# Seven block products of sums in place of eight, for six pairs of token tiles of an output product

## The chip, the cores and the metric

The kernel runs on one core of a Trainium2 chip. The metric is the device time of one execution in microseconds (us); lower is better. The engines are named as in the profile: PE (TensorE), DVE (VectorE), ACT (ScalarE), POOL (GpSimd) and SP (SyncE, which here issues nearly all DMA transfers).

## What is computed

Two request groups (1024 tokens each, width 1024) go through one encoder layer with shared weights:

```python
proj = x @ w_in                      # x: layer norm of the input
q_da, k_da, v_da, g_da, b_cv, c_cv, h_cv, g_cv, q_mx, g_mx = jnp.split(proj, idx, axis=-1)
o_da = diff_attention(q, k, v, lam, lam_init, subln_g) * jax.nn.silu(g_da)
o_cv = b_cv * short_conv(c_cv * h_cv, conv_w) * jax.nn.silu(g_cv)
o_mx = memory_attention(q_mx, mem, w_mem_kv) * jax.nn.silu(g_mx)
out = jnp.concatenate([o_da, o_cv, o_mx], axis=-1) @ w_o
return layer_norm(ALPHA * x + out, ln_g, ln_b)
```

The change is about the last two lines: the product of the mixed heads (1024 tokens x 1024, per group) with `w_o` (1024 x 1024), the residual, and the closing layer norm.

## The kernel before

Every product is taken in three passes over operands split into a high part (fp32r) and a low part (what the high part leaves out): high x high, high x low, low x high. A token tile is 128 rows, a column half 512, and a contraction block (kb) 128.

The program is written out by hand in one order. `Flow` keeps a planned clock: each piece of PE work adds its estimate with `fl.pe(ns)`, and `after(ns, fn)` puts work of the other engines into the program when that clock has come far enough. Each engine's queue then holds its instructions in the order in which they were put there. Twenty attention jobs (two groups x four heads and one memory attention x two query halves) form the frame. Between their steps the `Fillers` list supplies the projection tiles (`pQ`, `pK`, `pV`, `pG`, ... at L435 to L437), and at its end the output products. PE has eight PSUM banks: four for scores and transposes, two that the fillers take in turn (`next_bank`), one for small extras (`bank`), one for the attention output (`po`).

The output part before (L866 to L956):

- `load_wo(n, gap)` fetches column half n of `w_o` in eight blocks `woraw`. POOL makes the high part `woh` (L157), DVE the low part `wol` (L160). Half 0 is loaded in the last job, half 1 when the last projection tile is done.
- `Out(g, t)` is one token tile; there are sixteen. `load` fetches the mixed heads `mraw` (512 KB) and the input rows `xr` (512 KB), both through SP. `prepare` splits `mraw` (ACT `mixh` at L908, DVE `mixl`). `residual` makes ALPHA times the normed input: ACT at L915, DVE at L916, two adds on POOL at L919.
- `passes(n, kb)` issues three matmuls 128x128 by 128x512 into `pout` (L927): 8 blocks x 2 halves x 3 = 48 per tile, 768 in all. After a half, DVE adds the residual (L930) and takes `bn_stats` (L933).
- `finish` closes a tile: DVE `bn_aggr` (L941), POOL the reciprocal root in two small operations (L943, L944), DVE `centre` (L948) and `scale` (L951) for each half, and the store, through SP for the first four tiles and through ACT's queue for the others.

```python
for ti, (a, b) in enumerate(((self.mh, wh), (self.mh, wl), (self.ml, wh))):
    T.matmul(self.ps, a[:, kb, :], b, start=kb == 0 and ti == 0, stop=kb == KB - 1 and ti == 2)
```

## Time and profile before

| | |
|---|---|
| time, median of 3 runs (lowest to highest) | 1214.94 us (1214.8 to 1216.38) |
| profiled execution, its own time | 1216.07 us |
| span of the profiled execution, first to last instruction | 1214.2 us |
| mean granted TensorE clock over the span | 0.996 of 2.4 GHz |
| busy: PE, DVE, ACT, POOL | 1175.9, 803.0, 426.2, 415.7 us |
| DMA | 182.61 MB, mean 150 GB/s |

PE is busy for 97% of the span, so the place to look at is the 3% in which it is not, and the number of matmuls. A page's busy times say how much an engine did; whether its work costs time is told by the idle time of PE and by what ended it.

### The profile page before, as it was taken

The numbers are of one execution on the slowest core, as the hardware profiler recorded it, in microseconds if no ns is written. First come the engines' busy times: TensorE is split into PE (matmuls) and PEld (weight loads), VectorE is DVE, ScalarE is ACT, GpSimd is POOL, SyncE is SP. The second block draws the span as 40 slices with busy tenths as digits, with TensorE's granted clock in tenths as the row PEclk, the third lists the DMA queues.
The fourth block names the chain that finished last, engine by engine and source line by source line (L and its number), as shares of the span: only waits on it lengthen the run. The fifth ranks groups of instructions, "written<-read, shape, count | busy, mean of one in ns | idle before, by whom it ended". The sixth has DMA issues, their size and how long they took to land.

```text
span 1214.2 us, 15653 instructions
## 1 busy us (share of the span) xinstructions
PE 1175.9 (97%) x5881; PEld 922.0 (76%) x5881; DVE 803.0 (66%) x1156; ACT 426.2 (35%) x703; POOL 415.7 (34%) x466
## 2 busy tenths in 40 slices
PE   8899999999999999999999999999999998899997
PEld 6677777777777777788777777777777877788885
DVE  4779857666677675543766765665655456887776
ACT  4624333334233334334344333433433344111220
POOL 4754423352234430322311113023110346445443
PEclk9999999999999999999999999999999999999999
DMA  8366336433644389753321212312322368354341
GB/s 325 102 230 217 145 130 208 153 144 113 216 156 156 122 281 309 260 191 128 133 71 64 92 40 95 100 68 92 111 78 74 127 222 294 99 196 144 133 145 52
DMA packets 83644, 182.61 MB, mean 150 GB/s; under 512 B 7713, under 2 KB 26353, under 8 KB 83441
## 3 DMA queue, kind: packets, MB, share of 16 engines
q1 hardware_dynamic: 80112, 175.33, 41.3%
q10 hardware_dynamic: 3456, 6.29, 1.3%
q8 instruction: 46, 0.75, 0.3%
q14 instruction: 30, 0.24, 0.1%
HBM read 119.69 MB, written 61.91 MB: 150 GB/s over the span
## 4 chain that ended last, share of the span: by engine, by line
PE 75%; DVE 11%; POOL 3%; issue 3%; ACT 3%; DMA 3%; SPq 0%; POOLq 0%; DVEq 0%; ACTq 0%
PE pout L927 13%; PE ps L678 7%; PE pt L736 5%; PE po L764 3%; PE pG L435 2%; PE po L766 2%; PE po L765 2%; PE pG L437 2%; PE pG L436 2%; DVE mx L685 2%; PE pQ L435 2%; PE pQ L437 2%; PE pQ L436 2%; ACT e L686 2%; PE pV L435 2%
## 5 line engine op out<-in xcount | busy, mean ns | idle before, releaser
L686 ACT ACTIVATE e<-ps,mx 128x1024 f32<-128x1024 f32 x128 | 142.8, 1116 | 295.8 <-DVE mx L685 295.6
L685 DVE TENSOR_REDUCE mx<-ps 128x1 f32<-128x1024 f32 x128 | 150.6, 1218 | 87.7 <-PE ps L678 87.7
L160 DVE TENSOR_TENSOR tl<-pt,th 128x1024 fp32r<-128x1024 f32 x80 | 97.3, 1217 | 11.7 <-ACT th L742 11.6
L927 PE MATMUL pout<-woh,mixh 128*128 128x512 f32 x256 | 100.6, 393 | 0.0
L927 PE MATMUL pout<-woh,mixl 128*128 128x512 f32 x256 | 100.4, 392 | 0.0
L927 PE MATMUL pout<-wol,mixh 128*128 128x512 f32 x256 | 100.2, 391 | 0.0
L742 ACT ACTIVATE th<-pt 128x1024 fp32r<-128x1024 f32 x80 | 82.3, 1029 | 42.6 <-PE pt L736 42.1
L694 DVE SCALAR_TENSOR_TENSOR e<-e,ssum,e 128x1024 f32<-128x1024 f32 x64 | 87.9, 1373 | 0.0
L919 POOL TENSOR_TENSOR xr<-xr,lnrow 128x512 f32<-128x512 f32 x32 | 55.7, 1758 | 68.9 <-DVE xr L916 68.8
L476 POOL TENSOR_TENSOR sw<-sw,ropet 128x512 f32<-128x512 f32 x32 | 41.7, 1302 | 90.7 <-DVE sw L470 88.1
L736 PE MATMUL pt<-ident,e 128*128 128x128 f32 x512 | 66.8, 274 | 4.8 <-ACT e L686 4.8
L736 PEld LDWEIGHTS pt<-ident,e 128*128 128x128 f32 x512 | 58.9, 141 | 16.1 <-ACT e L686 8.1
L678 PE MATMUL ps<-kh,qh 64*128 64x512 f32 x256 | 62.8, 444 | 5.4 <-DVE tl L160 5.4
L722 POOL TENSOR_SCALAR em<-em,rm 128x256 f32<-128x256 f32 x64 | 31.9, 517 | 83.2 <-DVE rm L720 76.4
L160 DVE TENSOR_TENSOR wl<-wraw,wh 128x1024 fp32r<-128x1024 f32 (+1 forms) x33 | 43.0, 1303 | 23.7 <-POOL wh L157 13.8
L908 ACT ACTIVATE mixh<-mraw 128x1024 fp32r<-128x1024 f32 x16 | 17.0, 1061 | 114.6 <-PE pout L927 97.6
L764 PE MATMUL po<-th,vh 128*128 128x512 f32 x128 | 56.7, 443 | 0.0
L927 PEld LDWEIGHTS pout<-woh,mixl 128*128 128x128 f32 x256 | 48.3, 189 | 10.8 <-DVE mixl L160 0.6
L678 PE MATMUL ps<-kl,qh 64*128 64x512 f32 x256 | 54.6, 392 | 1.6 <-DVE kl L479 1.5
L927 PEld LDWEIGHTS pout<-wol,mixh 128*128 128x128 f32 x256 | 48.4, 189 | 10.0
L927 PEld LDWEIGHTS pout<-woh,mixh 128*128 128x128 f32 x256 | 48.4, 189 | 9.9
L678 PE MATMUL ps<-kh,ql 64*128 64x512 f32 x256 | 53.9, 390 | 0.0
(284 smaller groups left out, 3069.9 us busy)
## 6 DMA issues: line engine op xcount, KB each, us to landing
wp<-w SPq DMA_DIRECT2D x80, 512.0 KB, 4.3
wraw<-in_wt SPq DMA_DIRECT2D x32, 512.0 KB, 4.4
w<-wh SPq DMA_DIRECT2D x28, 512.0 KB, 5.4
w<-wl SPq DMA_DIRECT2D x28, 512.0 KB, 3.8
mraw<-mix SPq DMA_DIRECT2D x16, 512.0 KB
xr<-in_x SPq DMA_DIRECT2D x16, 512.0 KB, 6.5
out<-xr ACTq DMA_DIRECT2D x24, 256.0 KB, 2.1
x<-in_x SPq DMA_DIRECT2D x8, 512.0 KB, 4.4
```

What stands on the lines that cost most here:

```text
L160: (eng or V).tensor_tensor(out, x, hi.bitcast(F32), op=ALU.subtract)
L435: T.matmul(ps, wh[:, k], hh, start=kb == 0, stop=False)
L436: T.matmul(ps, wh[:, k], hl, start=False, stop=False)
L678: T.matmul(ps[c][:, n], q[r, qt * P:(qt + 1) * P], k[r, n], start=i == 0, stop=i == 2)
L685: V.tensor_reduce(mx[:, c:c + 1], ps[c], AX.X, ALU.max, negate=True)
L686: A.activation(e[c], ps[c], AF.Exp, bias=mx[:, c:c + 1], accum_out=sm[:, c:c + 1])
L694: V.scalar_tensor_tensor(e[0], e[1], st, e[0], op0=ALU.mult, op1=ALU.add)
L736: T.transpose(pt[:, u * HS + i * P:u * HS + (i + 1) * P], self.tiles[i][:, (b + u) * P:(b + u + 1) * P], const["ident"])
L742: A.activation(th, pt, AF.Copy)
L764: T.matmul(self.po, vh[:, k, :], th[:, c], start=k == 0, stop=False)
L919: after(2200 + 2000 * n, lambda c=c: G.tensor_tensor(xt[:, c], xt[:, c], ab[:, c], op=ALU.add))
L927: T.matmul(self.ps, a[:, kb, :], b, start=kb == 0 and ti == 0, stop=kb == KB - 1 and ti == 2)
```

## The change

The first four token tiles of group 0 keep the old form. The other twelve are taken as six pairs. With the 2 x 2 blocks A11, A12 (first tile, contraction halves), A21, A22 (second tile) and B11 to B22 (quarters of `w_o`), a pair needs seven block products P0 to P6 of twelve matmuls each, four of them with sums of blocks:

- `Pair.ORDER` names the seven products, operand, bank and, where there is one, the sum of `w_o` blocks: P0 A11 x B11 into bank `pa`; P1 S12 x T1 into `pb`; P2 A12 x B21 into `pa` again; P3 S12 x T0 into `pc`; P4 S34 x T2 into `pd`; P5 S34 x B22 into `pc`; P6 A22 x T3 into `pd`.
- P0 alone is needed too, so ACT copies `pa` to `s1` before P2 goes on adding into that bank. ACT also copies `pc` to `s5` after P3. DVE and POOL put the results together in `xr`.
- The sums of the token blocks are made by POOL (`sums`), their splits by ACT and DVE (`splits`), for the next pair during the present one.
- The sums of the `w_o` blocks, and the split quarters of `w_o`, are made in the course of jobs 11 and later by POOL (`park_wo`, `park_unit`) and parked in DRAM; `load_wo` and `load_sums` fetch both parts, with no split. The residuals are made there too and parked (`park_residual`).
- The closing norm of a pair's second tile (`mixed`) is done in one ACT pass with a scale and a bias (POOL makes the bias `nbo` in two more small operations), a multiply on DVE and an add on POOL. The last pair's second tile has the old form.
- Stores go through SP, but for the last pair's.

```diff
+RP = 162000
...
+    def park_unit(n, x, dst):
+        hi = sb([P, HS], F32R, ("kmh", "kml")[n % 2], "whi")
+        hi_of(hi, x)
+        after(300, lambda: G.tensor_tensor(x, x, hi.bitcast(F32), op=ALU.subtract))
+        def out():
+            dma(dst[0], hi.bitcast(F32))
+            dma(dst[1], x)
+        after(3800, out)
...
+    def park_residual(i):
...
+        after(4000, lambda: A.activation(x, x, AF.Identity, bias=st[:, 0, t:t + 1], scale=st[:, 1, t:t + 1]))
+        after(6000, lambda: V.tensor_tensor(x, x, resid["g"], op=ALU.mult))
+        for n in range(2):
+            c = slice(n * HS, n * HS + HS)
+            after(7600, lambda n=n, c=c: G.tensor_tensor(x[:, c], x[:, c], resid["b"][n], op=ALU.add))
+        after(10800, lambda: dma(r_d[g][t * P:(t + 1) * P, :], x))
     def load_wo(n, gap):
         def step(kb):
-            raw = sb([P, HS], F32, "ev", "woraw")
-            dma(raw, wo[kb * P:(kb + 1) * P, n * HS:(n + 1) * HS])
...
+            for t, src in zip(W[kb, n], wo_d[kb, n]):
+                dma(t.bitcast(F32), src)
...
+    def normalise(g, t, y, bs, mixed):
+        mv = sb([P, 2], F32, "small", "mvo")
+        V.bn_aggr(mv, bs)
...
+        G.tensor_tensor(nb, mv[:, 0:1], ve, op=ALU.mult)
+        G.tensor_scalar(nb, nb, -1.0, 1.0, op0=ALU.mult, op1=ALU.mult)
+        after(1500, lambda: A.activation(y, y, AF.Identity, bias=nb, scale=ve))
+        for n, c in enumerate(halves):
+            after(2800 + FD * n, lambda n=n, c=c: V.tensor_tensor(y[:, c], y[:, c], W["lg"][n], op=ALU.mult))
+            after(4000 + 1700 * n, lambda n=n, c=c: close(n, c))
...
+    class Pair:
+        ORDER = (("A", 0, 0, None), ("S12", 1, 1, 1), ("A", 1, 0, None), ("S12", 0, 2, 0), ("S34", 0, 3, 2), ("S34", 1, 2, None),
+                 ("A22", 0, 3, 3))
...
+            for n, (x, y) in enumerate(((ah, b[0]), (ah, b[1]), (al, b[0]))):
+                T.matmul(ps, x, y, start=first and n == 0, stop=kk == 3 and n == 2, skip_group_check=i in (2, 5, 6))
...
+        def after_product(self, i):
+            if i == 0:
+                self.s1 = sb([P, HS], F32, "ev", "s1")
+                A.activation(self.s1, f[0], AF.Copy)
+            if i == 1:
+                self.u = sb([P, HS], F32, "ev", "u")
+                V.tensor_tensor(self.u, f[1], self.s1, op=ALU.add)
+                G.tensor_tensor(x1[:, hi], x1[:, hi], self.u, op=ALU.add)
+                G.tensor_tensor(x2[:, lo], x2[:, lo], self.u, op=ALU.add)
+            if i == 2:
+                V.tensor_tensor(x1[:, lo], f[0], x1[:, lo], op=ALU.add)
+                stat_of(x1, 0, self.bs[0])
+            if i == 3:
+                self.s5 = sb([P, HS], F32, "ev", "s5")
+                A.activation(self.s5, f[2], AF.Copy)
+                G.tensor_tensor(x2[:, hi], x2[:, hi], self.s5, op=ALU.add)
+                if nxt:
+                    nxt.sums()
+                    nxt.splits("A")
+            if i == 4:
+                V.tensor_tensor(w, f[3], self.u, op=ALU.add)
+                V.tensor_tensor(x2[:, hi], x2[:, hi], w, op=ALU.add)
+                stat_of(x2, 1, self.bs[1])
+                if nxt:
+                    after(1500, lambda: nxt.splits("S12"))
+            if i == 5:
+                V.tensor_tensor(x1[:, hi], f[2], x1[:, hi], op=ALU.add)
+                stat_of(x1, 1, self.bs[0])
+                normalise(self.g, 2 * self.p, x1, self.bs[0][0], False)
+            if i == 6:
+                V.tensor_tensor(x2[:, lo], f[3], x2[:, lo], op=ALU.add)
+                stat_of(x2, 0, self.bs[1])
+                normalise(self.g, 2 * self.p + 1, x2, self.bs[1][0], nxt is not None)
+                if nxt:
+                    nxt.splits("S34")
+                    nxt.splits("A22")
...
-    outs = [Out(g, t) for g in range(2) for t in range(8)]
+    outs = [Out(0, t) for t in range(4)]
+    pairs = [Pair(0, 2), Pair(0, 3)] + [Pair(1, p) for p in range(4)]
...
+        if n == 11:
+            for r in range(4):
+                after(6000 + 38000 * r, lambda r=r: park_wo(r))
+            for i in range(16):
+                after(RP + 6300 * i, lambda i=i: park_residual(i))
```

How the instructions then stand is read from the built program; line numbers in these rows are those of the changed kernel. First ACT, from the end of one pair into the next (`a2h` is the split of A22, `xr<-xr,nbo,veo` the norm of the second tile, `s<-pa` and `s<-pc` the copies after P0 and P3, `ah` and `sh` splits for the pair after):

```order
L1114 ACTIVATE a2h<-mraw 128x512
L1031 ACTIVATE xr<-xr,nbo,veo 128x1024
L1143 ACTIVATE s_10211<-pa 128x512
L1154 ACTIVATE s_10272<-pc 128x512
L1114 ACTIVATE ah<-mraw 128x1024
L1114 ACTIVATE sh<-sums 128x512 x4
```

The norm of a pair's second tile stands ahead of the copy of the next pair's P0. Then PE, at the passage from P0 over P1 to P2, with the engines that a matmul waits for:

```order
L1133 MATMUL pa<-wol_0_9266,ah 128x512
L1133 MATMUL pa<-woh_0_9265,al 128x512
L1133 MATMUL pb<-wot,sh 128x512 [waits Activation_49]
L1133 MATMUL pb<-wot,sh 128x512
L1133 MATMUL pb<-wot,sh 128x512 [waits DVE_49]
L1133 MATMUL pb<-wot,sh 128x512 x9
L1133 MATMUL pa<-woh_0_9297,ah 128x512 [waits Activation_49]
```

The first matmul of P2 goes into the bank that P0 filled, and waits for ACT. DVE, from the split of the next pair's A (after P3) to the statistics of the second tile (after P6):

```order
L161 TENSOR_TENSOR al<-mraw,ah 128x1024
L1161 TENSOR_TENSOR w_10468<-pd,u 128x512
L1162 TENSOR_TENSOR xr<-xr,w_10468 128x512
L996 BN_STATS bso<-xr 128x6
L161 TENSOR_TENSOR sh<-sums,sh 128x512 x2
L1167 TENSOR_TENSOR xr<-pc,xr 128x512
L996 BN_STATS bso<-xr 128x6
L1000 BN_AGGR mvo<-bso 128x2
L1014 SCALAR_TENSOR_TENSOR xr<-xr,mvo,lg 128x512 x2
L1017 SCALAR_TENSOR_TENSOR xr<-xr,veo,lb 128x512 x2
L1171 TENSOR_TENSOR xr<-pd,xr 128x512
```

The first tile's norm (four operations, L1014 and L1017) stands ahead of the add that follows P6 (L1171). Last SP, around the fetch of the sums of `w_o` for the first pair (`wot` is a sum's two parts, `mraw` and `xr` the next pair's):

```order
L978 DMA mraw<-mix_1_81 128x8x128 x2
L990 DMA xr<-res_87 128x1024 x2
L473 DMA out<-xr 128x512 x4
L967 DMA wot<-wot 128x2x512 x12
L978 DMA mraw<-mix_1_81 128x8x128 x2
```

Twelve transfers of 512 KB (three sums of four) stand ahead of the second pair's mixed heads.

## Rows read from the trace of the kernel before

**Rows 1.** The page: busy times, and the chain that ended last.
```profile
PE 1175.9 (97%) x5881; PEld 922.0 (76%) x5881; DVE 803.0 (66%) x1156; ACT 426.2 (35%) x703; POOL 415.7 (34%) x466
...
PE 75%; DVE 11%; POOL 3%; issue 3%; ACT 3%; DMA 3%; SPq 0%; POOLq 0%; DVEq 0%; ACTq 0%
```
**Rows 2.** Stretches: us, busy PE, PEld, DVE, ACT, POOL (count), clock, DMA share, GB/s.
```profile
660.00:760.00 100.00, 100.00 (x520) 77.64 (x519) 63.36 (x94) 35.84 (x55) 18.21 (x22) 1.00 0.21 75
...
965.00:1056.00 91.00, 82.89 (x414) 66.01 (x413) 59.96 (x71) 32.67 (x62) 46.46 (x56) 0.96 0.61 208
...
1100.00:1120.00 20.00, 20.00 (x90) 16.57 (x89) 14.65 (x20) 4.39 (x4) 8.79 (x7) 1.00 0.35 126
```
**Rows 3.** The chain that ended last, from 1056 us: start, us, what.
```profile
1056.38 149.81 PE pout L927 x660
...
1206.21 0.70 DVE xr L930
...
1207.67 0.22 DVE mvo L941
...
1207.97 0.75 POOL veo L943
...
1209.77 0.75 DVE xr L951
```
**Rows 4.** Groups by line, shapes apart: count, busy us, mean ns, idle before and releaser.
```profile
L915 ACT ACTIVATE xr<-xr,st 128x1024 f32<-128x1024 f32 x16 | 19.7, 1231 | 0.0
...
L908 ACT ACTIVATE mixh<-mraw 128x1024 fp32r<-128x1024 f32 x16 | 17.0, 1061 | 114.6 <-PE pout L927 97.6 <-DMA mraw<-mix 17.0
...
L788 ACT ACTIVATE sq<-po 128x512 f32<-128x512 f32 x16 | 9.6, 600 | 0.0
...
L237 POOL TENSOR_TENSOR st<-nm,st 128x1 f32<-128x1 f32 x16 | 7.5, 470 | 1.3
L801 POOL TENSOR_SCALAR ms<-ms 128x4 f32<-128x4 f32 x16 | 5.1, 321 | 1.4
```
**Rows 5.** Groups by line of DVE: nearest operations to the new ones.
```profile
L160 DVE TENSOR_TENSOR mixl<-mraw,mixh 128x1024 fp32r<-128x1024 f32 x16 | 21.0, 1312 | 0.0
L916 DVE TENSOR_TENSOR xr<-xr,lnrow 128x1024 f32<-128x1024 f32 x16 | 19.5, 1221 | 10.4 <-ACT xr L915 8.3 <-POOL lnrow L995 2.1
...
L160 DVE TENSOR_TENSOR wol<-woraw,woh 128x512 fp32r<-128x512 f32 x16 | 16.3, 1030 | 7.6 <-POOL woh L157 7.6
...
L160 DVE TENSOR_TENSOR vl<-vt,vh 128x512 fp32r<-128x512 f32 x16 | 13.0, 811 | 19.0 <-POOL vh L157 19.0
...
L160 DVE TENSOR_TENSOR kml<-kmraw,kmh 128x512 fp32r<-128x512 f32 x2 | 1.4, 682 | 0.0
```
**Rows 6.** DVE in order of time, 1109 to 1113 us: one tile's norm.
```profile
1109.99 1.41 DVE L948 SCALAR_TENSOR_TENSOR xr<-xr,mvo,lnrow 128x512 f32<-128x512 f32 x2
1111.85 1.41 DVE L951 SCALAR_TENSOR_TENSOR xr<-xr,veo,lnrow 128x512 f32<-128x512 f32 x2 [0.44 <-POOL veo L944]
```
**Rows 7.** PE in order of time, 1005 to 1062 us: idle before, releaser.
```profile
1008.88 0.50 PE L760 MATMUL po<-tl,vmst 128*128 128x512 f32 x1 [3.98 <-DVE tl L160]
...
1036.82 0.50 PE L760 MATMUL po<-tl,vmst 128*128 128x512 f32 x1 [2.41 <-DVE tl L160]
...
1055.41 0.50 PE L760 MATMUL po<-tl,vmst 128*128 128x512 f32 x1 [0.65 <-DVE tl L160]
```
**Rows 8.** Stretches behind the first two of these; columns as in rows 2.
```profile
1009.00:1014.00 5.00, 5.00 (x19) 4.15 (x20) 2.23 (x3) 1.71 (x3) 0.39 (x1) 0.66 1.03 337
1037.00:1042.00 5.00, 5.00 (x20) 4.07 (x21) 4.90 (x7) 0.94 (x2) 1.92 (x3) 0.66 0.52 178
```
**Rows 9.** Two instructions of POOL: ns minimum, median, maximum; first and last start.
```profile
L919 POOL TENSOR_TENSOR xr<-xr,lnrow x32: 1284/1734/2279, 1020.4 to 1195.6; 128x512 f32<-128x512 f32 x32
...
L157 POOL TENSOR_SCALAR vh<-vt x16: 610/619/625, 53.9 to 855.0; 128x512 fp32r<-128x512 f32 x16
```
**Rows 10.** A stretch in which DVE and POOL had more to do; columns as in rows 2.
```profile
300.00:400.00 100.00, 97.63 (x483) 75.68 (x481) 67.33 (x92) 31.19 (x47) 36.17 (x35) 1.00 0.48 167
```

More of the change, by code (lines that the diff above doesn't have):

```diff
@@ L386, in __init__ @@
             self.i = self.k = self.bank = 0
-            self.tiles = [(it[0], it[1]) if it[0] not in ("do", "out") else None for it in items]
+            self.tiles = [(it[0], it[1]) if it[0] not in ("do", "out", "pair") else None for it in items]
         def done(self):
@@ L412, in step @@
             name, j, g, half = self.items[self.i]
+            if name == "pair":
+                pairs[j].step(self.k // 4, self.k % 4)
+                self.k += 1
+                if self.k == 28:
+                    self.i += 1
+                    self.k = 0
+                return True
             if name == "out":
-                outs[8 * g + j].passes(half, self.k)
+                outs[j].passes(half, self.k)
                 self.k += 1
@@ L910, in prepare @@
             self.late = after(1500, lambda: lo_of(self.ml, self.mr, self.mh))
-        def residual(self):
-            xt, st = self.xt, stats[self.g]
-            ag, ab = W["rows"][0:2]
-            A.activation(xt, xt, AF.Identity, bias=st[:, 0, self.t:self.t + 1], scale=st[:, 1, self.t:self.t + 1])
-            after(1000, lambda: V.tensor_tensor(xt, xt, ag, op=ALU.mult))
-            for n in range(2):
-                c = slice(n * HS, n * HS + HS)
-                after(2200 + 2000 * n, lambda c=c: G.tensor_tensor(xt[:, c], xt[:, c], ab[:, c], op=ALU.add))
         def passes(self, n, kb):
@@ L965, in items @@
                 for n in names.split() for half in halves]
-    both, last, tail = (0, 1), "G3 QM0 QM1 GM0 GM1", "GM0 GM1 CB1 CG1"
+    both, last, ends = (0, 1), "G3 QM0 QM1 GM0 GM1", "GM0 GM1 CB1 CG1"
     plan = [
@@ L990, in start_out, with do @@
         outs[1].load()
+        outs[0].residual()
         after(4000, outs[0].prepare)
-    def rows_out():
-        load_rows()
-        after(3000, lambda: [G.tensor_scalar(r, r, ALPHA, 1.0, op0=ALU.mult, op1=ALU.mult) for r in W["rows"][:2]])
-        after(4000, outs[0].residual)
-    def ahead(t, what, ns=0):
-        def go():
-            for w in what.split():
-                after(ns, getattr(outs[t], w)) if ns else getattr(outs[t], w)()
-        return ("do", go)
+    def do(fn, ns=0):
+        return ("do", (lambda: after(ns, fn)) if ns else fn)
@@ L1004, in encoder, with tail_done @@
+    tail = []
+    def tail_done():
+        assert tail, "the sums' buffers are not free yet"
     n_last = len(its) - 1
-    its[n_last:] = [("do", rows_out), its[n_last], ("do", load_rows), ("do", outs[1].prepare), ("do", lambda: load_wo(1, W1))]
-    its[n_last - 1:n_last - 1] = [("do", lambda: after(1500, start_out))]
+    its[n_last + 1:] = [do(outs[1].prepare), do(lambda: load_wo(1, W1)), do(lambda: load_sums(2, ("kh", "kl")))]
+    its[n_last - 1:n_last - 1] = [do(start_out, 1500)]
     until[-1] = len(its)
-    its += [ahead(2, "load"), ("out", 0, 0, 0), ahead(1, "residual"), ahead(2, "prepare", P2), ("out", 1, 0, 0), ahead(2, "residual"),
-            ahead(3, "load"), ("out", 2, 0, 0), ("out", 0, 0, 1), ahead(3, "prepare residual"), ahead(4, "load"),
-            ("out", 1, 0, 1), ("out", 2, 0, 1)]
@@ L1011, in encoder @@
-    for t in range(3, 16):
-        its += [("out", t % 8, t // 8, 0)]
-        if t < 15:
-            its += [ahead(t + 1, "prepare residual")]
-        if t < 14:
-            its += [ahead(t + 2, "load")]
-        its += [("out", t % 8, t // 8, 1)]
+    its += [do(outs[2].load), ("out", 0, 0, 0), do(outs[2].prepare, P2), do(outs[2].residual), ("out", 1, 0, 0), do(load_rows),
+            ("out", 2, 0, 0), ("out", 0, 0, 1), do(outs[3].load), ("out", 1, 0, 1), do(outs[3].prepare), do(pairs[0].load),
+            ("out", 2, 0, 1), do(tail_done), ("out", 3, 0, 0), do(lambda: load_sums(1, ("e0", "e0"))), do(lambda: load_sums(0, ("e0", "e0"))),
+            do(pairs[0].sums), do(lambda: pairs[0].splits("A"), 3000), do(lambda: pairs[0].splits("S12"), 4500),
+            do(lambda: pairs[0].splits("S34"), 6000), do(lambda: pairs[0].splits("A22"), 7000),
+            ("out", 3, 0, 1), do(lambda: load_sums(3, ("vh", "vl")))]
@@ L1018, in encoder @@
+    its += [("pair", i, 0, 0) for i in range(len(pairs))]
     fillers = Fillers(its)
@@ L1084, in encoder @@
     prev.av(3)
+    tail.append(True)
     while not fillers.done():
```

213 lines of the change are left out of this document (166 added, 47 removed).

## The prediction

> **What bounds the kernel now.** I read the page's busy times first, then the chain that ended last, then stretches of the span, then single rows of PE's neighbours. PE is busy 97% of the span, and three quarters of the chain that ended last lie on it [rows 1]. So the kernel is bound by PE nearly everywhere, and two things can move the time: the number of matmuls, and the idle time of PE. The stretches tell where the idle time is [rows 2]: none at 660 to 760 us and none in the output stage at 1100 to 1120 us, but 8.1 us (91 less 82.89) at 965 to 1056 us, where the attention ends and `w_o` is fetched and split. The end of the chain [rows 3] gives the price of a matmul in the output stage, 149.81 us / 660 = 0.227 us, and what follows a tile's last matmul: add and statistics on DVE, two small steps on POOL, then the scaling. Before, that tail of a tile holds nobody up, because no matmul waits for it. The reader is to ask of the change whether this still holds.
>
> **What it removes.** Twelve tiles took 12 x 48 = 576 matmuls; six pairs take 6 x 84 = 504. The 72 that go are worth 72 x 0.227 = **-16.3 us**, if PE stays without a wait.
>
> **The wait at a pair's border.** P2 adds into the bank of P0, and must wait until ACT has copied `pa`. On ACT that copy stands behind the norm of the last pair's second tile, and this norm hangs on P6 of that pair. So from the end of P6 the chain is: add, statistics, `ve`, `nbo`, norm, copy. From rows: add to the point where `ve` is there, 1209.77 - 1206.21 = 3.56 us [rows 3]; the two steps of `nbo`, not in the trace, between 0.2 and 1.4 us by the small steps of POOL, taken as 0.47 + 0.32 and 0.16 for two starts (the gap of 0.08 between 1207.89 and 1207.97) = 0.95 [rows 3, 4]; the norm 1.23, as the ACT pass with scale and bias, and the copy out of PSUM 0.60, as `sq` [rows 4], with 0.1 for starts. Sum 6.4 us. PE has P0 and P1 to do meanwhile: 24 x 0.227 = 5.4 us, of which 0.2 lie under the end of P6's last matmul. With an idle DVE, PE would thus wait some 1.2 us.
>
> DVE is not idle. Its queue has the whole norm of the first tile between the add after P5 and the add after P6: 3.56 us until `ve` is there, then two scalings of 1.41 together [rows 6], so 5.0 us, where P5 and P6 are 12 x 0.227 = 2.7 apart: 2.3 late. The add after P5 stands behind the work after P4: an add from PSUM (0.70), an add in SBUF (0.70), statistics (0.71) and two splits. A split of 128x512 took 0.68 to 1.03 us [rows 5]; at 0.81 each the sum is 3.7 for 2.7: 1.0 late (0.8 to 1.5). The work after P4 in turn stands behind `al`: copy 0.60, split 1.06 on ACT, 1.31 on DVE [rows 4, 5] make 3.0 for 2.7: 0.3 late. Together PE waits 1.2 + 2.3 + 1.0 + 0.3 = **4.8 us** at a border. I keep 1.2 and 5.5 as ends. No backlog is carried over, since DVE goes on while PE waits.
>
> A wait of that length also costs clock. After waits of 3.98 and 2.41 us the stretches show a mean granted clock of 0.66, after one of 0.65 us nothing of the kind [rows 7, 8]. Of each 5 us a third is missing, 1.7 us of work: part of each stretch ran at the lower level, 1.2 instead of 2.4 GHz. A border then costs 4.8 + 1.7 = 6.5 us. There are five borders between six pairs: **+32.5 us**. The Trainium skill (TensorE: Matmul & The Clock Gate, HAM oscillation — how this bites in real kernels) says that a loop in which PE waits in each round pays the slow start anew each round. The trace has only two such waits, both paid; were the later ones not to pay, the sum would be 8.5 us lower, at 1230.
>
> **The first pair.** SP has twelve transfers of 512 KB (sums of `w_o`) ahead of the second pair's mixed heads. The best rate seen is 337 GB/s at a DMA share of 1.03 [rows 8], so 6.3 MB take 18.7 us and the two of mixed heads 3.1 more, 21.8. P6 of the first pair comes 96 matmuls after the start of these fetches, also 21.8 us. But before P6 the new heads must pass ACT (1.06) and DVE (1.31), as `al` stands ahead of the add out of `pd` (0.70) that P6 waits for: 3.1 us and a landing, so 3.5 late, and again 1.7 for the clock: **+5.2** (0 to 8).
>
> **The end.** The last pair has the first tile's norm ahead of its last add too, so the tail starts **+2.3 us** later. Its other steps are those of rows 3.
>
> **The passage to the output.** The splits of `w_o` leave POOL and DVE (on DVE 16.3 us [rows 5]), and the residual's passes leave all three engines. PE's waits there, 3.98 + 2.41 + 0.65 [rows 7], and two slow starts of 1.7 make 10.4 us that could go. Against it stands twice the volume for `w_o` (8.4 MB for 4.2) and 2.1 MB of the sums, in a stretch that already moved 208 GB/s [rows 2]. I take half, **-5** (0 to -10.4).
>
> **The parking.** From job 11 on, for some 270 us (by the diff's planned clock 162 + 16 x 6.3 = 263), POOL gets 48 sums and low parts, 32 high parts and 32 adds, at best 80 x 1.28 + 32 x 0.62 = 122 us [rows 9]; DVE gets 16 x 1.22 and ACT 16 x 1.23, some 20 us each [rows 4, 5]. PE has no idle time there now, because DVE is at 63% and POOL at 18% [rows 2]. After the change DVE stands near 70% and POOL near 60%. A stretch at 67% and 36% lost 2.4 us in 100 [rows 10], so over 270 us 6.4 at that level. The new steps lie between the old ones rather than on the path, so I take **+5**; the ends are nothing (all hidden) and 19.5 (the whole of DVE's 16 passes on the path).
>
> **The sum.** -16.3 + 32.5 + 5.2 + 2.3 - 5 + 5 = +23.7 us. Against the profiled execution's own 1216.07 this is 1239.8; that execution was 1.1 us above the median of the runs, so for a median I say **1239 us**.
>
> **Rivals.** *The border is covered* (faster). It decides at one point: whether the copy of `pa` is done within the 5.4 us of P0 and P1, or so little after that the clock stays up. That is so if ACT's queue let the copy, ready after P0, go ahead of the waiting norm, or if DVE came to the add after P6 without delay. For it: the same tail holds nobody up before. Against it: even with an idle DVE the rows make 6.4 us. The time: no wait gives -16.3 + 5.2 + 2.3 - 5 + 5 = -8.8, 1206 us; five waits of 1.2 without a slow start, -2.8, near 1212. The Trainium skill (PSUM — Partial Sum Buffer, Engine vs sequencer instructions) says that ScalarE's queue is strictly first in, first out, which leaves only the second way; no row here shows a ready ACT instruction behind a waiting one. *The parking starves the main part* (slower still). Rows show that DVE waited 19.0 us for POOL's 16 `vh` splits with a nearly idle POOL [rows 5]; now each can stand behind parked pieces of 1.9 us (1.28 + 0.62), and SP's queue holds stores that wait for POOL ahead of the weights that PE needs. Taken at its upper end, 19.5 for 5, and with nothing won at the passage, the sum is +23.7 + 14.5 + 5 = 43, about 1258. *The waits at the borders are there but pay no slow start*: 1230, within the first forecast's range.
>
> **Chances.** About 0.2%, 2.4 us, is what a measurement of this kernel can tell from no change. The forecast (borders wait, with or without the slow start) gets 0.78, the starved main part 0.13, the covered border 0.09, of which I count 0.06 as faster, 0.02 as no difference and 0.01 as slower. Within the forecast, low prices everywhere (a border of 4.7, nothing for the first pair, 10 won at the passage, 2 for the parking) would come to -16.3 + 23.5 + 2.3 - 10 + 2 = +1.5, 1216, so another 0.02 goes to no difference and 0.01 to faster. That makes 0.07 faster, 0.04 same, 0.89 slower. The range, 1221 to 1260, leaves out the covered border and the joint low ends below, and what lies beyond the starved case above.
>
> **What the profile would show.** Right: the first matmul of P2 waits for ACT's copy in five of six pairs, 3 to 6 us each, with stretches at half clock behind; 72 fewer matmuls; one wait for DVE before the first pair's P6; PE nearly without idle time up to 950 us. Wrong: PE without a wait in the pairs (then 1206 to 1212), idle time of PE over 10 us in all between 630 and 950 us, or waits for `w_o` or its sums, which I priced at nothing.

## The result, and the profile after

The changed kernel takes 1257.3 us (median of 4 runs, 1256.5 to 1263.0) against 1215.5 for the kernel before beside it: a ratio of 1.035, with a 95% interval of 1.032 to 1.039. The forecast was 1239 us, slower. Direction and main mechanism held; the sum came out 17 us too low (profiled execution 1256.5, forecast for it 1239.8).

The page of the changed kernel, busy times and the chain that ended last, to be held against [rows 1]:

```profile
PE 1181.1 (94%) x5809; PEld 918.7 (73%) x5809; DVE 818.7 (65%) x1166; ACT 450.7 (36%) x744; POOL 564.9 (45%) x593
...
PE 8%; POOL 6%; DVE 5%; DMA 4%; issue 4%; ACT 1%; SPq 0%; POOLq 0%; DVEq 0%; ACTq 0%
```

There are 72 matmuls fewer, and yet PE is busy 5 us longer, most of all because a part of them runs at half clock. The chain no longer lies on PE for three quarters. Three stretches (columns as in rows 2): the first answers to a line of [rows 2].

```profile
660.00:760.00 100.00, 98.72 (x510) 76.74 (x510) 65.42 (x92) 35.33 (x54) 69.47 (x66) 1.00 0.60 208
800.00:900.00 100.00, 92.56 (x459) 70.81 (x457) 66.27 (x86) 44.03 (x60) 56.45 (x49) 0.97 0.61 213
...
1082.00:1242.00 160.00, 133.31 (x506) 104.47 (x505) 100.16 (x141) 34.73 (x50) 93.42 (x82) 0.89 0.41 143
```

POOL's load rises from 18% to 69% at 660 to 760 us, as the prediction had it (near 60%), and PE loses 1.3 us there. At 800 to 900 us, where the residual is parked, it loses 7.4. In the pairs (the last line) the mean granted clock is 0.89. Where the time went is read from starts of PE's instructions: `pw` (16 small transposes of the attention's row sums, the last near its end) and `pout`, of the kernel before and then of the changed one (ns minimum/median/maximum; first to last start):

```profile
L810 PE MATMUL pw<-ident,rs x16: 270/272/276, 180.9 to 992.6; 128*4 128x128 f32 x16
L927 PE MATMUL pout<-woh,mixh x256: 387/389/632, 1018.7 to 1205.3; 128*128 128x512 f32 x128
```

```profile
L821 PE MATMUL pw<-ident,rs x16: 270/273/276, 180.6 to 1010.9; 128*4 128x128 f32 x16
L1063 PE MATMUL pout<-woh,mixh x64: 388/389/505, 1030.7 to 1083.3; 128*128 128x512 f32 x64
L1133 PE MATMUL pa<-woh,ah x48: 392/398/796, 1084.0 to 1232.1; 128*128 128x512 f32 x48
L1133 PE MATMUL pd<-wot,a2l x24: 393/398/628, 1107.1 to 1243.7; 128*128 128x512 f32 x24
```

With the start of the last matmul of the fourth tile of before (its 192nd output matmul, 1075.1 us) and the two spans (1214.2 and 1254.4) this splits the loss:

| stretch | before | after | difference | predicted |
|---|---|---|---|---|
| to the last `pw` (parking) | 992.6 | 1010.9 | +18.3 | +5 |
| from there to the end of four single tiles (passage) | 82.5 | 72.9 | -9.6 | -5 |
| twelve tiles, now six pairs | 130.7 | 159.9 | +29.2 | -16.3 + 32.5 + 5.2 = +21.4 |
| last matmul to the end | 8.4 | 10.7 | +2.3 | +2.3 |
| sum | 1214.2 | 1254.4 | +40.2 | +23.7 |

**The pairs.** PE's waits from 600 us on, changed kernel (us in total, times, longest):

```profile
PE pa L1133 <- ACT s L1143: 22.2, 5, 4.7
PE ps L689 <- DVE tl L161: 8.0, 7, 2.9
PE pt L747 <- ACT e L697: 7.1, 5, 1.9
PE pd L1133 <- DVE w L1161: 2.9, 1, 2.9
PE pb L1133 <- DMA wot<-wot: 1.6, 2, 0.9
```

The first line is the border: five waits for ACT's copy, 4.7 us each but the first. One border in order of time, all engines, with the steps of the predicted chain:

```profile
1168.52 0.68 DVE L1171 TENSOR_TENSOR xr<-pd,xr 128x512 f32<-128x512 f32 x1
...
1170.86 0.87 POOL L1003 TENSOR_TENSOR veo<-veo,mhalf 128x1 f32<-128x1 f32 x1
...
1172.09 0.19 POOL L1030 TENSOR_SCALAR nbo<-nbo 128x1 f32<-128x1 f32 x1
1172.32 1.24 ACT L1031 ACTIVATE xr<-xr,nbo,veo 128x1024 f32<-128x1024 f32 x1 [6.25 <-POOL nbo L1030]
...
1173.46 0.58 ACT L1143 ACTIVATE s<-pa 128x512 f32<-128x512 f32 x1
...
1174.09 0.80 PE L1133 MATMUL pa<-woh,ah 128*128 128x512 f32 x1 [4.70 <-ACT s L1143]
```

The add out of `pd` is followed by statistics, `veo`, `nbo`, the ACT pass and the copy, 5.5 us from the first to the last, and PE starts 0.05 us behind the copy. ACT stood idle for 6.25 us ahead of its pass, with the copy behind it in the queue. What follows each wait is the clock (the stretches behind that border):

```profile
1174.00:1179.00 5.00, 4.91 (x12) 3.85 (x13) 1.48 (x3) 0.04 (x1) 4.63 (x4) 0.50 0.94 329
1179.00:1182.00 3.00, 3.00 (x12) 2.41 (x11) 1.39 (x2) 0.00 (x0) 0.74 (x1) 0.79 0.23 87
```

Five us at the lower level and three at 0.79 are 2.5 + 0.6 = 3.1 us lost at this border. In the pairs there are six stretches at a clock of 0.50, one at the wait for `w` and one at each border. The last of them, and the sum of the six:

```profile
1228.10:1231.50 3.40, 2.84 (x7) 2.29 (x8) 1.90 (x3) 0.50 (x2) 2.57 (x2) 0.50 0.02 5
sum 34.00, PE 30.75 PEld 24.12 DVE 16.47 ACT 4.38 POOL 28.45; mean PE 5.12 PEld 4.02 DVE 2.74 ACT 0.73 POOL 4.74
```

In the last PE works for 2.84 us, so that border loses 1.4. In all six it works for 30.75 of 34 us, the rest is part of the waits. Half of 30.75, 15.4 us, is what the clock costs in the pairs, where five borders and the first pair were priced at 6 x 1.7 = 10.2. One thing more costs time: at full clock and without a wait the matmuls of the pairs start 0.2323 us apart, those of the kernel before 0.2267, which makes 2.8 us over 504. No run shows why.

**The main part.** From 630 to 950 us PE waits 13.9 us in ten places, for DVE's `tl` and ACT's `e`; before it was 1.0 in one. These 12.9 us more, and 2.8 for a stretch at half clock that begins in the longest wait (845.8 to 852.6 us, with 5.7 us of work), make 15.7 of the 18.3 us. The longest place, DVE and then POOL in order of time:

```profile
839.56 2.04 DVE L948 TENSOR_TENSOR xres<-xres,ag 128x1024 f32<-128x1024 f32 x1 [3.53 <-ACT xres L947]
...
842.02 2.03 DVE L705 SCALAR_TENSOR_TENSOR e<-e,ssum,e 128x1024 f32<-128x1024 f32 x1
843.97 1.75 DVE L490 SCALAR_TENSOR_TENSOR kl<-rt,kh 128x512 fp32r<-128x512 f32 x1
845.64 1.21 DVE L161 TENSOR_TENSOR tl<-pt,th 128x1024 fp32r<-128x1024 f32 x1
```

```profile
839.23 1.29 POOL L833 TENSOR_TENSOR og<-og,rb 128x512 f32<-128x512 f32 x1 [1.75 <-DMA rb<-rd]
841.68 3.49 POOL L951 TENSOR_TENSOR xres<-xres,ab 128x512 f32<-128x512 f32 x2 [1.16 <-DVE r L702]
```

Two things meet here. DVE stands 3.53 us for ACT's pass over the residual, with `e`, `kl` and `tl` behind in its queue. And `xres`, `e` and `kl`, which read two operands from SBUF, take 2.04, 2.03 and 1.75 us while POOL adds, where `e` takes 1.37 and `kl` 0.69 on average in the kernel before, from 830 to 925 us. `tl`, with one operand from PSUM, takes its 1.21 here with POOL idle, but 28 of the 80 `tl` of this trace lie beside a POOL operation and take 1.20 to 1.23 us as well. PE then waits 2.9 us for `tl`, and half clock follows.

### The profile page after: what moved, and what is told of

Same layout as the page of the kernel before. It is cut to its first block, busy times and chain, and to the rows that moved or that the text cites. A ratio compares the mean times of both kernels' runs of the same rounds, so it can differ in the third digit from the quotient of the medians.

```text
span 1254.4 us, 16044 instructions
## 1 busy us (share of the span) xinstructions
PE 1181.1 (94%) x5809; PEld 918.7 (73%) x5809; DVE 818.7 (65%) x1166; ACT 450.7 (36%) x744; POOL 564.9 (45%) x593
## 5 line engine op out<-in xcount | busy, mean ns | idle before, releaser
L705 DVE SCALAR_TENSOR_TENSOR e<-e,ssum,e 128x1024 f32<-128x1024 f32 x64 | 92.9, 1452 | 0.0
L689 PE MATMUL ps<-kh,qh 64*128 64x512 f32 x256 | 67.2, 446 | 11.1 <-DVE tl L161 11.1
L951 POOL TENSOR_TENSOR xres<-xres,ab 128x512 f32<-128x512 f32 x32 | 47.0, 1490 | 46.2 <-DVE xres L948 24.5
L689 PEld LDWEIGHTS ps<-kh,qh 64*128 64x128 f32 x256 | 29.3, 185 | 40.8 <-issue 22.3
L158 POOL TENSOR_SCALAR wh<-wraw 128x1024 fp32r<-128x1024 f32 (+1 forms) x32 | 32.9, 1028 | 52.7 <-PE pG L447 12.3
L305 POOL TENSOR_TENSOR xt<-xt,shift 128x512 f32<-128x512 f32 x16 | 23.8, 1487 | 64.0 <-DVE xt L302 22.1
L777 PE MATMUL po<-tl,vh 128*128 128x512 f32 x128 | 51.3, 401 | 0.0
L776 PE MATMUL po<-th,vl 128*128 128x512 f32 x128 | 51.0, 398 | 0.0
L488 POOL TENSOR_TENSOR rt<-rt,sw 128x512 f32<-128x512 f32 x32 | 46.1, 1442 | 2.5
L1133 PE MATMUL pa<-woh,ah 128*128 128x512 f32 x48 | 23.8, 495 | 22.2 <-ACT s L1143 22.2
```

Source lines behind the costliest of these rows:

```text
L689: T.matmul(ps[c][:, n], q[r, qt * P:(qt + 1) * P], k[r, n], start=i == 0, stop=i == 2)
L705: V.scalar_tensor_tensor(e[0], e[1], st, e[0], op0=ALU.mult, op1=ALU.add)
L776: T.matmul(self.po, vl[:, k, :], th[:, c], start=False, stop=False)
L777: T.matmul(self.po, vh[:, k, :], tl[:, c], start=False, stop=end)
L951: after(7600, lambda n=n, c=c: G.tensor_tensor(x[:, c], x[:, c], resid["b"][n], op=ALU.add))
L1133: T.matmul(ps, x, y, start=first and n == 0, stop=kk == 3 and n == 2, skip_group_check=i in (2, 5, 6))
```

## The experiments

All ratios below are to the kernel before, run beside each on the same chip. "First output matmul" is the first start of `pout`; "the pairs" is the time from the first matmul of the six pairs to the last (159.7 us in the changed kernel).

### The order on ACT, and the form of the norm

Run e1_norm_after_copy:

```diff
-        after(1500, lambda: A.activation(y, y, AF.Identity, bias=nb, scale=ve))
+        after(4500, lambda: A.activation(y, y, AF.Identity, bias=nb, scale=ve))
-            after(2800 + FD * n, lambda n=n, c=c: V.tensor_tensor(y[:, c], y[:, c], W["lg"][n], op=ALU.mult))
-            after(4000 + 1700 * n, lambda n=n, c=c: close(n, c))
+            after(5800 + FD * n, lambda n=n, c=c: V.tensor_tensor(y[:, c], y[:, c], W["lg"][n], op=ALU.mult))
+            after(7000 + 1700 * n, lambda n=n, c=c: close(n, c))
```

> The normalise of each pair's second tile is emitted 3 us later (its ACT pass, the two lg products and the two lb additions behind it), so that ACT's queue holds the copy of the next pair's first product (tile s, L1143) ahead of the ACT pass (L1031). Nothing else is changed. Theory Q (the five waits at the borders come from the order in ACT's queue alone): the 22.2 us of PE's pa <- ACT s L1143 fall below 4 us, the half-clock stretches at 1122 to 1228 us go with them (about 17 us lost in them), and the time is about 1257 - 22 - 14 to 17 = 1218 to 1222 us. Theory L (POOL and DVE are too full in a pair: 17.4 and 17.2 us of work against 20.3 us of PE's): the wait comes back on other tiles of the border, pb (for the split sh) and pd (for w), with 2 to 4 us per pair and its half clock, and the time is 1235 to 1248 us. If the order of ACT had nothing to do with it: 1255 to 1259 us.

Measured: 1231.1 us, ratio 1.012 (1.010 to 1.014); the pairs take 132.9 us, 26.8 less. Its largest waits from 600 us on:

```profile
PE ps L689 <- DVE tl L161: 8.4, 7, 3.6
PE pd L1133 <- DVE w L1161: 8.4, 4, 2.8
```

The line of `pa` is gone, all five waits with it: the queue's order made them. (Two products on DVE and two additions on POOL moved with the pass; in the changed kernel, too, they come behind the copy and can't have held it up.) The time lies between the two theories, as some of the gain comes back as waits of `pd` for DVE's reading of the fifth product, `w`, three more than in the changed kernel, with two stretches at half clock in the pairs where that has six.

Run e2_norm_on_dve_late:

```diff
-                normalise(self.g, 2 * self.p + 1, x2, self.bs[1][0], nxt is not None)
+                normalise(self.g, 2 * self.p + 1, x2, self.bs[1][0], False, nxt is not None)
...
+                d = late and ((5300, 6700))
-                after(FD * n, lambda n=n, c=c: centre(n, c))
-                after(FD * (2 + n), lambda n=n, c=c: scale(n, c))
+                after((d[0] if d else 0) + FD * n, lambda n=n, c=c: centre(n, c))
+                after((d[1] if d else 2 * FD) + FD * n, lambda n=n, c=c: scale(n, c))
```

> The second tile of each pair is normalised in the old form (two DVE centre and two DVE scale operations; no ACT pass, no nbo, no two lb additions on POOL) and all four operations are emitted late, behind the next pair's second product. POOL loses about 3.4 us per pair (2 x 1.49 + 2 x 0.19), DVE gains 1.6 us (4 x 0.75 - 2 x 0.69). Theory Q (ACT's queue order alone): within 4 us of the run with the norm behind the copy, both 1218 to 1222 us. Theory L in the form that POOL is what is too full: 8 us or more below that run, 1222 to 1232 us against 1235 to 1248. Theory L in the form that DVE is too full: slower than that run, 1245 to 1255 us.

Measured: 1229.8 us, ratio 1.011 (1.009 to 1.013), pairs 134.3 us. It is within 1.3 us of the last run, as theory Q says of the two, but neither is at Q's level. The 8 us between the runs that L asked for if POOL is too full did not come, nor the loss if DVE is; but this run took 3.4 us per pair from POOL and gave 1.6 to DVE at once, so that a gain and a loss may have cancelled, and it can't rule out that each counts. (Runs e10 and e11 below show that each does.) What is left is one wait, `pd` for `w`, 9.1 us in 5.

### The parking, each half left out

Run e3_no_residual_parking:

```diff
-            for i in range(16):
-                after(RP + 6300 * i, lambda i=i: park_residual(i))
...
-            dma(x, r_d[g][(2 * p + j) * P:(2 * p + j + 1) * P, :])
+            dma(x, X[g][(2 * p + j) * P:(2 * p + j + 1) * P, :])
```

> The 16 passes that park the residual are left out; the output stage loads the raw inputs in their place (the scaling of the residual is left out of what is computed). The output stage is as in the changed kernel. Theory R (two thirds of what the main part lost comes from the residual parking: ACT waits in order for its loads, DVE behind ACT, slower DVE operations beside POOL's additions): the first output matmul comes at 1018 to 1021 us, not 1030.7, and the time is 1243 to 1247 us. Rival W (the sums of w_o on POOL are the larger part): first output matmul at 1025 to 1028 us, time 1251 to 1255 us.

Run e4_no_wo_sums:

```diff
     def park_wo(r):
-        def block(t, kb, n):
...
+        dst = [wo_d[kb, n, s] for kb in (r, r + 4) for n in range(2) for s in range(2)]
+        dst += [wt_d[i, r, s] for i in range(4) for s in range(2)]
+        for i, d in enumerate(dst):
+            src = wo[(r + 4 * (i % 2)) * P:(r + 4 * (i % 2) + 1) * P, 0:HS]
+            after(2200 * i, lambda d=d, src=src: dma(d, src))
```

> The parking of w_o is left out as computation: the blocks are copied from DRAM to DRAM as they are (no sums, no splits, no work on POOL, DVE or ACT's side; the products get wrong operands of the same shape), the residual parking stays. Theory R: the first output matmul comes 4 to 6 us earlier (1025 to 1027 us) and the time is 1251 to 1254 us. Rival W: it comes 10 us or more earlier and the time is 1240 to 1247 us. If both parts only cost together (each alone hides in what slack there is), this run and the one without the residual parking gain more together than the 11.7 us between the two kernels' first output matmuls (1030.7 against 1018.7 us).

Measured: 1246.0 us (ratio 1.024, 1.023 to 1.026) and 1248.2 us (1.026, 1.024 to 1.028). The last `pw`, and the first output matmul, without the residual's parking and then without the sums:

```profile
L821 PE MATMUL pw<-ident,rs x16: 270/273/276, 180.8 to 999.6; 128*4 128x128 f32 x16
L1063 PE MATMUL pout<-woh,mixh x64: 389/389/503, 1019.8 to 1073.0; 128*128 128x512 f32 x64
```

```profile
L821 PE MATMUL pw<-ident,rs x16: 270/272/276, 180.7 to 1002.5; 128*4 128x128 f32 x16
L1040 PE MATMUL pout<-woh,mixh x64: 389/389/495, 1022.6 to 1075.0; 128*128 128x512 f32 x64
```

Against 1010.9 the residual's parking costs 11.3 us and that of `w_o` 8.4, together 19.7, where the table has 18.3: the two add up, and the +5 was too little for either alone. The remark in the second expectation, that a sum above 11.7 would mean that they cost only together, was mistaken: the two first output matmuls are 12.0 us apart (1030.7 less 1018.7), and that is what is left of 18.3 after 6 us are won between the last `pw` and the first output matmul. Theory R's number held for the first run; for the second neither did.

### What in the residual's parking costs

Run e5_no_residual_adds (the two additions left out) and run e6_adds_off_the_chain (as many, on other operands):

```diff
-            after(7600, lambda n=n, c=c: G.tensor_tensor(x[:, c], x[:, c], resid["b"][n], op=ALU.add))
+            pass
```

```diff
-            after(7600, lambda n=n, c=c: G.tensor_tensor(x[:, c], x[:, c], resid["b"][n], op=ALU.add))
+            after(7600, lambda n=n, c=c: G.tensor_tensor(resid["b"][n], resid["g"][:, c], resid["b"][n], op=ALU.subtract))
```

> The two POOL additions of each residual pass (x + scaled bias row) are left out of the computation; load, ACT pass, DVE product and store stay. Two theories for the 11 us that the residual parking costs. Theory O (order: ACT waits in its queue for a load that waits for the store two passes before, and DVE's product waits for ACT): leaving the additions out also lets the store, and so the next load, go some 3 us earlier, so the first output matmul comes at 1021 to 1025 us (1030.7 in the changed kernel) and the time is 1247 to 1251 us. Theory C (contention: DVE's operations with two inputs from SBUF, 1339 ns for e without the residual parking and 1644 ns with it, are slowed by POOL's additions): the same gain, and e back at 1.35 to 1.42 us. This run alone does not separate the two; it is the pair of the next one.

> POOL does as many operations of the same shape at the same places as the residual's additions, but on the two bias rows alone (the addition is left out of the residual), so that the store does not wait for them. Theory O: as the run without the additions, first output matmul at 1021 to 1025 us, time 1247 to 1251 us, and e stays at about 1.6 us. Theory C: as the changed kernel, first output matmul at 1029 to 1031 us, time 1255 to 1258 us. In between, the share of each is the distance to the two.

Run e7_residual_retimed, with nothing left out:

```diff
-                after(RP + 6300 * i, lambda i=i: park_residual(i))
+                after(162000 + 6700 * i, lambda i=i: park_residual(i))
...
-        after(6000, lambda: V.tensor_tensor(x, x, resid["g"], op=ALU.mult))
+        after(6500, lambda: V.tensor_tensor(x, x, resid["g"], op=ALU.mult))
-            after(7600, lambda n=n, c=c: G.tensor_tensor(x[:, c], x[:, c], resid["b"][n], op=ALU.add))
+            after(8100, lambda n=n, c=c: G.tensor_tensor(x[:, c], x[:, c], resid["b"][n], op=ALU.add))
-        after(10800, lambda: dma(r_d[g][t * P:(t + 1) * P, :], x))
+        after(10000, lambda: dma(r_d[g][t * P:(t + 1) * P, :], x))
```

> The residual passes as in the changed kernel, nothing left out, with other times of emission: a pass every 6.7 us instead of 6.3, the DVE product 2.5 us behind the ACT pass instead of 2.0, the additions 0.5 us later, the store 0.8 us earlier in SP's queue. Theory O: ACT's waits for the load (9.1 us) and DVE's for ACT (12.4 us) fall to less than half, first output matmul at 1023 to 1026 us, time 1249 to 1252 us. Theory C: the same work on POOL and DVE, no gain beyond 2 us, 1255 to 1258 us.

Measured: 1250.4 us (ratio 1.028, 1.027 to 1.030), 1254.8 (1.031, 1.030 to 1.033) and 1251.2 (1.028, 1.027 to 1.030); first output matmul at 1023.6, 1027.4 and 1023.7 us. From 800 to 960 us, the waits of ACT and DVE and the group of `e` on DVE, in the changed kernel, then in the run with the additions off the chain, then in the retimed run:

```profile
ACT xres L947 <- DMA xres<-in_x: 14.7, 6, 5.6
DVE xres L948 <- ACT xres L947: 13.2, 6, 3.9
L705 DVE SCALAR_TENSOR_TENSOR e<-e,ssum,e 128x1024 f32<-128x1024 f32 x12 | 19.5, 1626 | 0.0
```

```profile
L705 DVE SCALAR_TENSOR_TENSOR e<-e,ssum,e 128x1024 f32<-128x1024 f32 x12 | 20.6, 1716 | 0.0
```

```profile
ACT xres L947 <- DMA xres<-in_x: 11.2, 8, 2.3
DVE xres L948 <- ACT xres L947: 3.4, 4, 1.3
L705 DVE SCALAR_TENSOR_TENSOR e<-e,ssum,e 128x1024 f32<-128x1024 f32 x12 | 20.8, 1730 | 0.0
```

Of the 7.1 us that the additions cost in the first output matmul, 3.3 go when they leave the chain and 3.8 only when they leave POOL; so both theories hold a share. (By the medians of the time it is 2.5 and 4.4 of 6.9: the profiled execution of run e6 is the fastest of its four.) But the retimed run gains 7.0 us with `e` as slow as ever (1.73 us). So slow operations need not cost time while DVE does not stand still. Of the two waits that theory O named, ACT's for its load fell by a quarter only, and DVE's for ACT from 13.2 to 3.4 us, so it is the second that went with the time.

### What is left in the pairs

Run e8_late_norm_and_split joins the late norm on DVE and the retimed residual, and moves `al`:

```diff
-                    nxt.splits("A")
+                    nxt.splits("A", 2700)
...
-                lo_of(lo[:, c], x, hi[:, c])
+                low = lambda c=c, x=x: lo_of(lo[:, c], x, hi[:, c])
+                after(gap, low) if gap else low()
```

> The run with the late norm on DVE (1229.8 us), with the residual passes retimed as in the run before, and with the low parts of the next pair's first operand (al, one 128x1024 DVE operation of 1.47 us) emitted 2.7 us later, behind DVE's reading of the fifth product (w). Theory Q (the waits of pd <- DVE w that are left, 9.1 us in 5, come from the place of al ahead of w): they fall below 3 us, their half clock (three stretches of 3.41 us) goes, the pairs take 118 to 124 us instead of 134.3, and the time is 1211 to 1219 us. Theory D (DVE is full in the pairs, 19.2 us busy of each 20 in that run): the wait moves to another tile (pa for al, pb for sh), the pairs stay at 131 to 135 us, and only the parking's share is gained: 1222 to 1228 us (1229 if that has no share either).

Measured: 1224.3 us, ratio 1.007 (1.005 to 1.008), pairs 135.2 us. Theory D's numbers, but not its sign: the wait did not move to another tile, it stayed where it was (8.5 us in 5), so `al` was not what made it.

Run e9_wo_sums_spread, on the base of run e8; it also starts the parking of `w_o` 2 us earlier, which the expectation does not name:

```diff
                 G.tensor_tensor(b22, b22, b12, op=ALU.subtract)
-                G.tensor_tensor(b12, b12, b11, op=ALU.subtract)
-                G.tensor_tensor(t2, b22, b11, op=ALU.add)
-                G.tensor_tensor(b21, b21, t2, op=ALU.subtract)
+                after(1500, lambda: G.tensor_tensor(b12, b12, b11, op=ALU.subtract))
+                after(3000, lambda: G.tensor_tensor(t2, b22, b11, op=ALU.add))
+                after(4500, lambda: G.tensor_tensor(b21, b21, t2, op=ALU.subtract))
...
-                    after(4500 + 2600 * i, lambda i=i, x=x, dst=dst: park_unit(i, x, dst))
+                    after(6000 + 3200 * i, lambda i=i, x=x, dst=dst: park_unit(i, x, dst))
...
-            after(19500 + 4000 * i, alone)
+            after(24000 + 4000 * i, alone)
...
-                after(6000 + 38000 * r, lambda r=r: park_wo(r))
+                after(4000 + 38000 * r, lambda r=r: park_wo(r))
```

> The run with the late norm, the late split and the retimed residual (1224.3 us, first output matmul at 1022.2 us), with the sums of w_o emitted 1.5 us apart instead of four in a row, their split and store every 3.2 us instead of 2.6, and the three single blocks 4.5 us later. Nothing is left out. Theory S (the w_o parking costs its 6 to 8 us because bursts of POOL operations stand in front of short POOL operations that DVE and PE wait for, as vh): first output matmul at 1016 to 1019 us, time 1217 to 1221 us. Rival T (it costs by its work as such, POOL's operations slowing DVE's, whenever they come): 1021 to 1023 us, time 1222 to 1226 us. The pairs take 134 to 136 us in either case.

Measured: 1221.4 us, ratio 1.004 (1.002 to 1.005), first output matmul at 1021.2 us. The longest wait of DVE for POOL's `vh` fell from 7.0 to 3.3 us. The time fell by 3, into the gap between the two forecasts; the first output matmul came only 1.0 us earlier than in run e8, within rival T's range. So bursts are at most a small part of what the sums of `w_o` cost, and the larger part stays unexplained.

Runs e10_less_dve_in_pairs and e11_less_pool_in_pairs each take some 7.5 us of work out of the pairs of run e8, one from DVE, one from POOL:

```diff
-                after((d[1] if d else 2 * FD) + FD * n, lambda n=n, c=c: scale(n, c))
+                after((d[1] if d else 2 * FD) + FD * n, lambda n=n, c=c: out(c) if d else scale(n, c))
```

```diff
-                G.tensor_tensor(x2[:, lo], x2[:, lo], self.u, op=ALU.add)
```

> The run with the late norm, the late split and the retimed residual, without the two scale operations of the second tile of five pairs (y stays centred and not scaled there; its stores go where they went): 10 DVE operations of 0.75 us less, 1.5 us of about 20 in each pair, nothing else. Theory D (DVE is full: 117 us busy in 131 us of the pairs): the pairs go from 135.2 to 123 to 129 us and the time from 1224.3 to 1212 to 1219 us. Rival H (the pairs are held by the chain of engines behind one another, POOL's sums, ACT's copy, DVE's low part, and not by DVE's sum of work): they stay at 133 to 136 us, time 1222 to 1226 us.

> The same run without one POOL addition in each pair (u is not added to the first half of the second tile): 6 POOL operations of 1.27 us less, nothing else. Theory D: the pairs stay at 133 to 136 us, time 1222 to 1226 us, since POOL is busy 81 of 131 us. Rival H: they fall with POOL's chain by 4 to 8 us, to 127 to 131 us, time 1216 to 1220 us.

Measured: 1216.0 us (ratio 1.000, 0.999 to 1.001), pairs 126.2; and 1219.3 us (1.002, 1.001 to 1.003), pairs 128.4. Each meets the forecast of the theory that the other contradicts. POOL had nearly 40% of its time free, and still 7.6 us less on POOL gave 6.8. So the two engines' work is not independent. The rows of run e9 at a border show how, DVE first and then POOL:

```profile
1147.90 1.42 DVE L1017 SCALAR_TENSOR_TENSOR xr<-xr,veo,lb 128x512 f32<-128x512 f32 x2 [0.44 <-POOL veo L1003]
...
1153.17 2.44 DVE L1014 SCALAR_TENSOR_TENSOR xr<-xr,mvo,lg 128x512 f32<-128x512 f32 x2
1155.54 3.47 DVE L1017 SCALAR_TENSOR_TENSOR xr<-xr,veo,lb 128x512 f32<-128x512 f32 x2
1158.93 0.68 DVE L1152 TENSOR_TENSOR xr<-pa,xr 128x512 f32<-128x512 f32 x1
```

```profile
1153.33 1.73 POOL L1149 TENSOR_TENSOR xr<-xr,u 128x512 f32<-128x512 f32 x1 [0.88 <-DVE u L1148]
1155.02 1.73 POOL L1150 TENSOR_TENSOR xr<-xr,u 128x512 f32<-128x512 f32 x1
1156.71 1.74 POOL L1157 TENSOR_TENSOR xr<-xr,s 128x512 f32<-128x512 f32 x1
1158.42 1.74 POOL L1092 TENSOR_TENSOR sums<-mraw 128x512 f32<-128x512 f32 x1
```

Two scale operations take 1.42 us with POOL idle and 3.47 beside its additions; POOL's additions take 1.73 there, where those of the changed kernel at 1176 to 1179 us took 1.28. The late norm had been put into a bad place. An add with an operand in PSUM (1158.93) keeps its 0.68 beside POOL.

Run e12_norm_between_pool_bursts moves DVE's work, on the base of run e9:

```diff
-                d = late and ((5300, 6700))
+                d = late if type(late) is tuple else late and ((0, 5300))
...
-                    after(1500, lambda: nxt.splits("S12"))
+                    after(2700, lambda: nxt.splits("S12"))
...
-                normalise(self.g, 2 * self.p, x1, self.bs[0][0], False)
+                normalise(self.g, 2 * self.p, x1, self.bs[0][0], False, (2000, 4000))
```

> The run with the w_o sums spread (1221.4 us, pairs 135.6 us), nothing left out, with the DVE operations of the pairs at other times: the second tile's two centre operations at once after its statistics, its scale operations 1.4 us earlier than there, the first tile's centre and scale operations 2.0 us and 2.4 us later, and the splits of S12 1.2 us later. Theory K (DVE and POOL slow each other when both work on SBUF: in the run before, two centre operations take 2.44 us and two scale operations 3.47 us beside POOL's additions, 1.42 us each pair without them, and POOL's additions 1.73 instead of 1.28 us): with the centre operations out of POOL's burst, and w ahead of what is left, the waits of pd for w (8.5 us in 5) fall below 3 us, the pairs take 126 to 130 us, and the time is 1213 to 1217 us, level with the kernel before or just under it. Rival D (the sum of DVE's operations decides, wherever they stand): the pairs stay at 133 to 137 us, time 1219 to 1223 us.

Measured: **1209.2 us** (1208.9 to 1211.8), ratio 0.9947 (0.9934 to 0.9961): half a per cent below the kernel before, and a little beyond what theory K gave. The pairs take 124.6 us. From 600 us on no wait of `pd` is left, and no wait is longer than 1.2 us:

```profile
PE ps L689 <- DVE tl L161: 3.6, 5, 1.1
PE pb L1135 <- DVE sh L161: 2.8, 5, 0.8
```

The six pairs as a whole, in run e9 and then here (columns as in rows 2):

```profile
1074.10:1209.90 135.80, 124.92 (x505) 96.84 (x504) 121.56 (x154) 27.99 (x44) 82.09 (x62) 0.96 0.48 164
```

```profile
1072.50:1197.50 125.00, 120.28 (x505) 93.38 (x503) 112.32 (x153) 27.23 (x43) 75.30 (x61) 1.00 0.52 178
```

The same work takes DVE 9.2 us less and POOL 6.8 less, so the two do slow each other less, and the granted clock is 1.00. DVE's busy share is 90% in both. Several emissions were moved at once (the second tile's centre and scale, the first tile's norm, the splits of S12), so the share of each, and that of less slowing against a better order, was not told apart.

## Why the prediction was right and where it was wrong

- **The border waits: right in mechanism, and in size with some luck.** 4.8 us forecast at each of five, 4.7 measured at four and 3.5 at the first. Two errors cancel: from the add after P6 to the end of the copy it took 5.5 us, not 6.4 (the two steps of `nbo` together some 0.5, not 0.95), and that add began 4.7 us behind the end of P6 (at 1163.85 in the border shown), not 2.3 + 1.0 + 0.3 = 3.6. Against the 5.5 us that PE then has P0 and P1 to do, a chain of 5.5 means that an idle DVE would have about covered the border, which the prediction's 6.4 ruled out. (An estimate from these rows; no run tested it.) The chain was the one named, and run e1 shows that the place of the copy behind the norm makes the wait. The Trainium skill (PSUM — Partial Sum Buffer, Engine vs sequencer instructions), cited for ACT's strict order, agrees: the copy out of `pa` sat behind a pass that waited 6.25 us. But the rival "border covered" was tied to a faster DVE or a queue that lets the copy go ahead; an emission 3 us later takes the wait off the copy too.
- **The clock behind a wait: mis-sized.** The step "of each 5 us a third is missing, 1.7 us of work", read off two waits, gave 10.2 us for five borders and the first pair. The six stretches at half clock cost 15.4. One border lost 1.4, another 3.1. The rule of the Trainium skill (TensorE: Matmul & The Clock Gate, HAM oscillation — how this bites in real kernels) that the prediction put beside the rows, a slow start paid anew in each round, holds at all five borders: each has its stretch at 0.50.
- **The first pair: about right.** 3.5 us for DVE and nothing for the sums' transfers were forecast; 2.9 and 1.6 came.
- **The sum of the pairs.** -16.3 + 22.2 + 2.9 + 1.6 + 15.4 + 2.8 = +28.6, measured +29.2; 0.6 us are not assigned. The forecast was +21.4. The clock makes 5.2 of the difference, and 2.8 come from a term that the forecast had put at nothing: it took a matmul of the pairs at the price of one before, 0.227, and each starts 0.0056 us later.
- **The passage: right in kind, mis-sized.** I took half of 10.4; 9.6 was won. The long waits at 1009 and 1037 us [rows 7], with the low clock behind them [rows 8], are gone; one of 0.6 us for DVE is left from 950 us to the pairs. Twice the volume for `w_o` cost 0.3 us of waits.
- **The parking: the step that failed.** "The new steps lie between the old ones rather than on the path, so I take +5": it cost 18.3, near the upper end of 19.5. Taking the main part's loss from a stretch with POOL at 36% left out what came in at POOL's 56 to 69%: DVE's steps with two operands in SBUF slowed (`e` by a fifth), and new steps waited for one engine inside the queue of another. Runs e3 and e4 share it out, 11.3 and 8.4; run e7 shows that 7 us of the former are a matter of when the steps are emitted. What makes the latter is largely open after run e9. The prediction had named over 10 us of idle PE between 630 and 950 us as a sign that it was wrong, and 13.9 came.
- **The end: right**, 2.3 us.
- **The rival "parking starves the main part"** gave 1258, and 1257.3 came, but the match of the sums is luck: it had nothing won at the passage, where 9.6 were, and the borders' clock at the low price. Its parking term, 19.5, was near the 18.3. Of its mechanism a part is seen: one wait of DVE for POOL's `vh` took 6.9 us.

## What to carry to other kernels

An operation that waits long must not stand in an in-order queue ahead of a short copy for which PE waits: emitting it a little later was worth 26 us here. Price a wait of PE with the clock behind it, and from more than one example. Before work is moved to POOL "because it is idle", look at what DVE does at that moment: POOL's additions and DVE's operations with two operands in SBUF take longer together, so place POOL's beside DVE's reads of PSUM instead, and ask of each parked step who stands behind it in each queue.
